# A hybrid decoder block on one core: a fifth pair of gates by seven products, six direct gates as filling, accumulating stores for the heads' second halves, and the keys of the linear attention in ScalarE's queue

## The chip, the cores and the metric

The kernel runs on one core of a Trainium2 chip, in one launch. A core has five engines, each with an instruction queue of its own that is worked off in order: TensorE (PE in the profile; loading its weights is shown apart as PEld), VectorE (DVE), ScalarE (ACT), GpSimd (POOL) and SyncE (SP). DMA transfers are asked for from the queues of SP, ACT and POOL and then run beside the engines. An instruction waits for what it needs by semaphores; all that stands behind it in its queue waits too.

The metric is the device time of the launch in microseconds (us); the number given for a kernel is the median of several runs.

## The reference

One layer of a decoder block on 1024 positions of width 1024, in float32. Cut to what matters here:

```python
xn = rms_norm(h, norm_mix_g)
proj = xn @ w_in                # sb_q, sb_k, sb_v, g_q, g_k, g_v, g_r, g_a, gate_sb, gate_gla
o_sb  = stick_breaking_attention(heads(sb_q, 8), heads(sb_k, 8), heads(sb_v, 8))
o_gla = gla_chunked(heads(g_q, 4) * GLA_DK ** -0.5, heads(g_k, 4), heads(g_v, 4), log_a)
o_gla = rms(o_gla) * gla_norm_g * silu(g_r)
y = (sigmoid(gate_sb + b_gate[0]) * (o_sb @ w_branch_sb)
     + sigmoid(gate_gla + b_gate[1]) * (o_gla @ w_branch_gla))
h = h + y @ w_out
hn = rms_norm(h, norm_ffn_g)
a, g = split(hn @ w_ffn_in)     # 2 x 2816 columns
h = h + (gelu(causal_conv3(a)) * g) @ w_ffn_out
out = rms_norm(h, norm_final_g)
```

The two merge gates (`gate_sb`, `gate_gla`) have 1024 channels each. The kernel holds a projection transposed, 128 channels on the partitions and 1024 positions along, so the gates are 16 blocks of 128 channels; the code calls one such block "a gate". Stick-breaking attention weighs position s for position t by a sigmoid times a product over the positions between, without a softmax. The gated linear attention (GLA) goes in chunks with a state from chunk to chunk; its "keys to the end of the chunk" (`k_to_end`, here `kt`) multiply the values to give the state's increments.

## The kernel before, in words

**Precision.** Each float32 operand of a large matrix product is held as two pieces, a high one of reduced precision and the rest: `split` (L121) is a copy with a cast on ScalarE (L122) and a subtraction on VectorE (`sub`, L113). A product is three matmuls (high by high, high by low, low by high); `mac` (L205 is the matmul in it) issues them for k blocks of 128 rows, into one PSUM bank of 128x512.

**Seven products.** A projection of two blocks of 128 channels can be done by one level of the seven-product scheme: `fast` (L235) takes pairs of channel blocks, builds four differences of their weight quarters, turns seven weight quarters into pieces, does seven products of 4 x 3 = 12 matmuls against prepared sums of `xn` (the dictionary `xq`), and adds the products up on VectorE. Done directly, one gate is 2 halves of the positions x 8 blocks of rows x 3 = 48 matmuls and needs no additions.

**Stages.** By the time at which they run in the profile: (1) load, norm and values, to about 150 us. (2) The pairs of projections by seven products, to about 343 us; their list is `project_pairs` (L589), and its last entries are the gate pairs, `N_GATES`/2 = 4 of them. A gate that is ready goes through a sigmoid and is stored to DRAM (`gate_d`). (3) Stick-breaking attention, `attend` (L883), to about 537 us. (4) GLA, `gated` (L1047), with the first branch projection `branch` (L1072) between its steps, to about 605 us. (5) The second branch, the output projection and the FFN's first product, to about 1290 us. (6) The FFN's second product in four quarters (`phase`, L1334), with the final norm of the last rows in `fourth_done` (L1417).

**Attention and its filling.** For each head `attend` yields blocks of 128x128 weights: `weigh` does the scores on PE, the sigmoid on ScalarE (L830) and a scan on VectorE (L833); `turn_weights` transposes up to four blocks on PE (L842) and splits them into pieces; `gather` multiplies by the values (L871). A gather covers one head and 256 positions, so there are 32, four to a head. Its result has two halves of 64 partitions (from the high and the low piece of the values) that are still to be added. ScalarE moves it out of PSUM with a bias (L877, two rows), and SP stores the two halves to two places of `osb_d` (L879). When the first half of the positions is complete for all heads, `heads` (L847) loads eight tiles back, adds them in pairs on VectorE (L119) and splits the four sums into `ob`, the operand of the first branch projection; for the second half of the positions the same is called inside GLA.

Between the attention's pieces PE is given gates to do directly: `gates` (L686) yields after each group of 6 matmuls, and the loop over `attend` (L1143 on) asks for one such group each time that a number of blocks has been yielded: `FILL` = 6 in the first three quarters of the blocks, 4 in the last. At the end of `attend` a drain empties its queues; there each yield counts for 2 blocks. What is left of the gates runs out after `fetch_rest`, in one go (`fill(gate_steps, 128)`). With `N_GATES` = 8 there are 16 - 8 = 8 gates of this kind. Three of them (`N_HALVES`) have their second halves of the positions done at the very end, and before those three halves `fetch_gated` asks for GLA's values, queries and inverse keys.

**Order around attention's end.** After the loop the program does `branch(0, ...)` up to its first stop, which loads the first two pieces of the branch weights (`in_w_branch_sb_dram`, two DMAs of 512 KB in POOL's queue, L181) and splits them; then `fetch_rest` (L956) loads the keys `kt` for two pairs of heads (L962, 512 KB each, in POOL's queue); then the last gates run. GLA starts with `states`, whose matmul (L970) is the first to read `kt`. The program fixes the order in each engine's queue, except that a priority offset (`LATER`) lets the scheduler that lays out the queues move gate matmuls later. Tiles come from pools with a fixed number of buffers (`t2`: 11 of 128x512; `t4`: 14 of 128x1024), so a new tile waits until the old one in its buffer has been read for the last time.

## Time and profile before

| | |
|---|---|
| median of 3 runs | 1386.93 us (1386.27 to 1387.03) |
| the profiled execution: its time | 1386.67 us |
| the profiled execution: its span | 1384.8 us |
| mean granted TensorE clock | 0.997 |

The page's parts on stages, by windows of the trace (columns: us of the window, then for PE, PEld, DVE, ACT and POOL the busy us and in brackets the number of instructions, the granted TensorE clock, the DMA engines' busy share, GB/s):

```profile
0.00:150.00 150.00, 146.95 (x660) 117.24 (x661) 104.29 (x164) 63.52 (x120) 22.33 (x36) 0.99 0.46 151
150.00:343.40 193.40, 193.40 (x868) 159.94 (x866) 143.48 (x224) 100.77 (x149) 40.02 (x66) 1.00 0.62 184
343.40:537.00 193.60, 192.36 (x1183) 167.00 (x1181) 156.56 (x232) 125.92 (x305) 28.17 (x50) 1.00 0.68 176
537.00:605.00 68.00, 67.99 (x422) 56.20 (x422) 43.61 (x88) 39.24 (x140) 14.19 (x22) 1.00 0.65 210
605.00:1290.00 685.00, 684.15 (x3048) 566.21 (x3048) 554.33 (x832) 267.37 (x438) 27.83 (x52) 1.00 0.49 163
```

How to read what is shown of the profile, here and in the prediction: "L205 PE MATMUL bank<-t,t" is the group of PE's matmuls at line 205 of the kernel, from two tiles named `t` into a PSUM bank; then come the tile's shape, "x" and the count, the busy us, the mean ns of one, and the idle us of the engine just before them with what ended it. In a row of the timeline, the start and the length in us stand first, then the engine ("SPq" is SP's queue), and in square brackets an idle time ahead of it and what released it. The chain of waits follows the work that ended last back to the start. Line numbers are those of the kernel before; behind the changed places, the changed kernel's are lower by 3 to 5 around attention and GLA (L966 of the changed kernel is L970 of the one before, L872 is L877, L958 is L962).

### The profile page before, as it was taken

Reading aid. Unit: us, or ns where it says so; the run is one execution under the profiler, and the core shown is the slowest. Engines: PE = TensorE matmul, PEld = TensorE weight load, DVE = VectorE, ACT = ScalarE, POOL = GpSimd, SP = SyncE. Lnnn points to the kernel's source line nnn. Section 1 sums busy time; section 2 is a strip of 40 time slices with the busy share of each in tenths; the row PEclk is TensorE's granted clock in tenths of the full one; section 3 lists DMA queues with packets and bytes.
Section 4 is the critical chain, followed back from the end, with each engine's and each line's share of the span. In section 5 each row is a group of like instructions: output and inputs, shape, how many; then the busy total and the mean of one; then the engine's idle time right before and its main releaser. Section 6 shows DMA issues by size and latency. Waiting matters only on the chain.

```text
span 1384.8 us, 18329 instructions
## 1 busy us (share of the span) xinstructions
PE 1372.4 (99%) x6559; PEld 1138.8 (82%) x6559; DVE 1064.6 (77%) x1640; ACT 643.9 (46%) x1244; POOL 136.3 (10%) x233
## 2 busy tenths in 40 slices
PE   9999999999999999999999999999999999999997
PEld 6788888888888888888888788888888888888886
DVE  6388688874878877658348998998888977896765
ACT  7334445653766664724126443343333334454654
POOL 2002123101111002200000000000000000000000
PEclk9999999999999999999999999999999999999999
DMA  6335278448776567673325245554444537953332
GB/s 239 132 117 151 84 221 251 143 158 210 216 158 151 131 197 237 198 237 136 136 91 177 52 120 187 196 189 152 150 163 152 182 107 272 322 163 102 99 101 105
DMA packets 164108, 227.92 MB, mean 165 GB/s; under 512 B 10938, under 2 KB 105276, under 8 KB 163506
## 3 DMA queue, kind: packets, MB, share of 16 engines
q1 hardware_dynamic: 134944, 139.01, 33.0%
q0 software_dynamic: 22496, 73.73, 16.8%
q10 hardware_dynamic: 6578, 14.03, 2.7%
q8 instruction: 51, 0.84, 0.3%
q14 instruction: 39, 0.32, 0.1%
HBM read 160.28 MB, written 66.45 MB: 164 GB/s over the span
## 4 chain that ended last, share of the span: by engine, by line
PE 95%; DVE 3%; ACT 1%; issue 0%; DMA 0%; ACTq 0%; DVEq 0%
PE bank L205 58%; PE bank L1343 15%; PE bank L385 6%; PE bank L1210 6%; PE bank L871 3%; PE bank L828 2%; PE bank L842 2%; DVE t L113 2%; PE bank L494 1%; PE bank L340 1%; DVE t L119 1%; PE bank L562 1%; PE bank L1007 1%; PE bank L970 0%; PE bank L994 0%
## 5 line engine op out<-in xcount | busy, mean ns | idle before, releaser
L205 PE MATMUL bank<-t,t 128*128 128x512 f32 x3624 | 861.1, 393 | 0.9 <-DVE t L113 0.7
L205 PEld LDWEIGHTS bank<-t,t 128*128 128x128 f32 x3624 | 676.5, 188 | 143.1 <-DVE t L113 1.6
L113 DVE TENSOR_TENSOR t<-t,t 128x512 fp32r<-128x512 f32 (+3 forms) x655 | 434.6, 697 | 93.5 <-ACT t L122 87.2
L122 ACT CAST t<-t 128x512 fp32r<-128x512 f32 (+1 forms) x543 | 320.3, 627 | 325.4 <-DVE t L113 81.0
L119 DVE TENSOR_TENSOR t<-bank,t 128x512 f32<-128x512 f32 x266 | 179.3, 685 | 97.9 <-PE bank L205 54.9
L1343 PE MATMUL bank<-t,t 128*128 128x512 f32 x924 | 209.6, 389 | 0.0
L1343 PEld LDWEIGHTS bank<-t,t 128*128 128x128 f32 x924 | 173.5, 188 | 36.0
L113 DVE TENSOR_TENSOR t<-bank,t 128x512 fp32r<-128x512 f32 (+4 forms) x124 | 69.5, 574 | 27.5 <-ACT t L122 26.9
L1210 PE MATMUL bank<-t,t 128*128 128x512 f32 x384 | 88.8, 391 | 0.0
L1241 ACT ACTIVATE t<-t,vcol 128x1024 f32<-128x1024 f32 x22 | 27.4, 1245 | 127.5 <-DVE t L119 127.5
L113 DVE TENSOR_TENSOR t<-t 128x512 f32<-128x512 f32 x120 | 83.3, 701 | 4.1 <-DMA t<-in_w_ffn_in_dram 3.7
L1210 PEld LDWEIGHTS bank<-t,t 128*128 128x128 f32 x384 | 71.6, 188 | 14.6
L119 DVE TENSOR_TENSOR t<-t,t 128x512 f32<-128x512 f32 x115 | 75.5, 686 | 9.8 <-ACT t L628 8.6
L122 ACT CAST t<-bank 128x512 fp32r<-128x512 f32 (+3 forms) x120 | 60.3, 512 | 48.8 <-PE bank L842 26.8
L385 PE MATMUL bank<-t,t 128*128 128x512 f32 x336 | 77.9, 391 | 0.0
L385 PEld LDWEIGHTS bank<-t,t 128*128 128x128 f32 x336 | 62.7, 188 | 13.1 <-DVE t L113 0.2
L1243 DVE SCALAR_TENSOR_TENSOR t<-t,vcol,t 128x1023 f32<-128x1023 f32 (+1 forms) x44 | 56.3, 1279 | 14.1 <-ACT t L1241 13.9
L833 DVE TENSOR_TENSOR_SCAN t<-t,t 128x128 f32<-128x128 f32 (+1 forms) x64 | 51.6, 816 | 17.5 <-ACT t L830 17.2
L828 PE MATMUL bank<-t,t 128*128 128x128 f32 (+3 forms) x192 | 54.6, 369 | 0.0
L842 PE MATMUL bank<-ident,t 128*128 128x128 f32 x288 | 53.2, 273 | 0.0
L871 PE MATMUL bank<-t,t 128*128 128x256 f32 (+1 forms) x320 | 51.0, 276 | 1.2 <-ACT t L122 0.7
L830 ACT ACTIVATE t<-bank 128x128 f32<-128x128 f32 (+3 forms) x96 | 46.9, 507 | 7.2 <-DMA osb_d<-t 3.2
(164 smaller groups left out, 813.5 us busy)
## 6 DMA issues: line engine op xcount, KB each, us to landing
t<-in_w_ffn_in_dram SPq DMA_DIRECT2D x50, 512.0 KB, 5.1
t<-in_w_in_dram SPq DMA_DIRECT2D x43, 512.0 KB, 5.3
act_d<-t POOLq DMA_DIRECT2D x22, 512.0 KB, 5.8
t<-in_w_ffn_out_dram SPq DMA_DIRECT2D x22, 512.0 KB, 7.6
wsum_d<-t POOLq DMA_DIRECT2D x22, 512.0 KB, 4.5
t<-act_d SPq DMA_DIRECT2D x22, 512.0 KB, 5.9
t<-wsum_d SPq DMA_DIRECT2D x44, 256.0 KB, 3.1
t<-in_w_ffn_out_dram SPq DMA_DIRECT2D x33, 256.0 KB, 2.7
```

The source lines that it names most:

```text
L113: nc.vector.tensor_tensor(out=o, in0=a, in1=b, op=ALU.subtract)
L119: nc.vector.tensor_tensor(out=o, in0=a, in1=b, op=ALU.add)
L122: nc.scalar.copy(h, src)
L205: nc.tensor.matmul(pt, a[:, kk], b[:, kk], start=start and kk == 0 and m == 0, stop=stop and kk == k - 1 and m == 2)
L385: nc.tensor.matmul(pt, a[:, k % 4, t], b, start=k == 0 and m == 0, stop=k == NK - 1 and m == 2)
L828: nc.tensor.matmul(z[:, 0:w], q[:, a, e, ts_], kk[:, e, b0 * P:b1 * P], start=a == 0, stop=a == 1)
L833: nc.vector.tensor_tensor_scan(out=kr, data0=kr, data1=above[:, 0:w], initial=1.0, op0=ALU.mult, op1=ALU.max)
L842: nc.tensor.transpose(pt[:, b * P:(b + 1) * P], ke[:, b * P:(b + 1) * P], ident)
L871: nc.tensor.matmul(po[:, c0:2 * P], vt[b][:, head, :], a[b // 4][:, b % 4, c0:], start=(b == 0 and n == 0), stop=(b == nb - 1 and n == 1))
L1210: nc.tensor.matmul(pt, a[:, k % 4, t], b, start=(k == 0 and m == 0), stop=(k == NK - 1 and m == 2))
L1243: nc.vector.scalar_tensor_tensor(out=cv[:, i:], in0=av[:, :S - i], scalar=col(V_CW, (2 - i) * NF + f), in1=cv[:, i:], op0=ALU.mult, op1=AL ...
L1343: nc.tensor.matmul(pts[m][i], a[:, t], b, start=(k == 0 and x_ == 0), stop=(k == NH - 1 and x_ == 2))
```

## The change

Five things change together.

1. `N_GATES` goes from 8 to 10: a fifth pair of gates is done by seven products in stage 2, and six gates instead of eight are left for filling.
2. `FILL` goes from (6, 4) to (8, 5), and a yield of the drain counts for `FILL[1]` blocks, so that each is followed by one group of 6 gate matmuls while there are any.
3. The two halves of a gather's result go to the same place of `osb_d`: the first half by a plain store in SP's queue, the second by an accumulating store in POOL's queue, which adds to what the first has written and therefore waits until that one has landed. `heads` loads four tiles instead of eight and adds nothing.
4. The loads of the keys `kt` in `fetch_rest` go from POOL's queue to ScalarE's.
5. In `fourth_done` the squares are written to `spare8`, the products in place, and the output is stored from the rows of `hr`.

```diff
--- before.py
+++ after.py
@@ -36,7 +36,7 @@
 T2 = 11
 AWAKE = 3
 T4 = 14
-FILL = 6, 4
+FILL = 8, 5
 EACH = 0
 LATER = 25
 MORE = 1
@@ -54,7 +54,7 @@
 WAIT = 1, 1, 5, 4, 1
 PACES = 0, 0, 0, 1
 EARLY = 6
-N_GATES = 8
+N_GATES = 10
 AT_END = 51
 HEADS_AT = 2
 GROUP = 4, 2
@@ -847,19 +847,14 @@
     def heads(th):
 
         ob.append(quarter())
-        asked, added = deque(), deque()
+        asked = deque()
         for k in range(6):
             if k < 4:
-                asked.append((t2(), t2()))
-                for n, v in enumerate(asked[-1]):
-                    nc.sync.dma_start(v, osb_d[n * HALF + k * P:n * HALF + (k + 1) * P, th * HALF:(th + 1) * HALF])
+                asked.append(t2())
+                nc.sync.dma_start(asked[-1], osb_d[k * P:(k + 1) * P, th * HALF:(th + 1) * HALF])
             yield
             if k > 1:
-                split(*(a[:, k - 2] for a in ob[th]), added.popleft())
-            if k in range(1, 5):
-                a, b = asked.popleft()
-                add(a, a, b)
-                added.append(a)
+                split(*(a[:, k - 2] for a in ob[th]), asked.popleft())
             yield
 
     def gather(head, tp, ah, al):
@@ -875,8 +870,9 @@
             c = slice(n * P, (n + 1) * P)
             i = head * NT + 2 * tp + n
             nc.scalar.activation(o[:, c], po[:, c], AF.Identity, bias=vend[:, i:i + 1])
-        for n, r in enumerate(HALVES):
-            nc.sync.dma_start(osb_d[n * HALF + head * 64:n * HALF + (head + 1) * 64, tp * 2 * P:(tp + 1) * 2 * P], o[r])
+        dst = osb_d[head * 64:(head + 1) * 64, tp * 2 * P:(tp + 1) * 2 * P]
+        nc.sync.dma_start(dst, o[HALVES[0]])
+        nc.gpsimd.dma_start(dst, o[HALVES[1]], accum_op=ALU.add)
         if head == SBH - 1 and tp == 1:
             first_heads.append(heads(0))
 
@@ -934,7 +930,7 @@
                 gather(*late.popleft())
             for v in first_heads:
                 next(v, None)
-            yield 2
+            yield FILL[1]
         fill(*first_heads, 12)
 
     last_values()
@@ -959,7 +955,7 @@
         state.extend((v[:, 0], v[:, 1]) for v in small)
         for p in range(2):
             kt = t4()
-            nc.gpsimd.dma_start(kt, kt_d[p * P:(p + 1) * P, :])
+            nc.scalar.dma_start(kt, kt_d[p * P:(p + 1) * P, :])
             gla[p] += by(kt, NT), by(t4(), NT)
 
     def states(p, n0, n1):
@@ -1415,23 +1411,21 @@
             mul(row(4 + i, 1), row(4 + i, 1), gfin[0][:, HALF:])
 
     def fourth_done(i, p4):
-        r = row(4 + i, 0)
+        r, q = row(4 + i, 0), row(4 + i, 1)
         sub(r, r, p4)
-        o = spare[i % 2]
         a, b = ss[i]
-        nc.scalar.activation(o[:, :HALF], r, AF.Square, accum_out=b)
+        nc.scalar.activation(spare8[:, i], r, AF.Square, accum_out=b)
         add(a, a, b)
         nc.scalar.activation(b, a, AF.Sqrt, bias=eps, scale=1.0 / D)
         nc.vector.reciprocal(a, b)
-        nc.scalar.activation(o[:, HALF:], row(4 + i, 1), AF.Copy, scale=a)
-        nc.vector.scalar_tensor_tensor(out=o[:, :HALF], in0=r, scalar=a, in1=gfin[0][:, :HALF],
-                                       op0=ALU.mult, op1=ALU.mult)
+        nc.scalar.activation(q, q, AF.Copy, scale=a)
+        nc.vector.scalar_tensor_tensor(out=r, in0=r, scalar=a, in1=gfin[0][:, :HALF], op0=ALU.mult, op1=ALU.mult)
         t = slice((4 + i) * P, (5 + i) * P)
         if i < 3:
-            nc.gpsimd.dma_start(out[t, :], o)
+            nc.gpsimd.dma_start(out[t, :], hr[4 + i])
         else:
-            nc.sync.dma_start(out[t, :HALF], o[:, :HALF])
-            nc.scalar.dma_start(out[t, HALF:], o[:, HALF:])
+            nc.sync.dma_start(out[t, :HALF], r)
+            nc.scalar.dma_start(out[t, HALF:], q)
 
     for n, _ in enumerate(jobs):
         if n == 0:
```

Three places of the queues show what moves. In them "DMASW" in a wait stands for the landing of a transfer that POOL asked for, "DMAHW" for the landing of one that SP or ScalarE asked for, and PE, DVE and Activation for work of TensorE, VectorE and ScalarE.

POOL's queue from the end of attention to GLA's first state, before (`gv_d`, `qd_d` and `ki_d` are the operands that `fetch_gated` loads, `in_w_branch_sb_dram` the branch weights, `kt_d` the keys, L981 the scaling of the first state):

```order
L950 DMA t_965_4971<-gv_d 128x4x512 [waits PE_49]
L952 DMA t_964_4970<-qd_d 128x1024 [waits DMASW4_49,PE_49]
L953 DMA t_964_4970<-ki_d 128x1024 [waits DMASW5_49]
L181 DMA t_1027_5307<-in_w_branch_sb_dram 128x4x256 [waits DMASW6_49,DMAHW6_49,DVE_49,PE_49]
L181 DMA t_1030_5315<-in_w_branch_sb_dram 128x4x256 [waits DMASW7_49,DMAHW0_49,DVE_49,PE_49]
L962 DMA t_1035_5325<-kt_d 128x1024 [waits DMASW0_49,PE_49]
L962 DMA t_1037_5328<-kt_d 128x1024 [waits DMAHW3_49,DMAHW1_49,DMAHW4_49,DMASW1_49,PE_49]
L981 TENSOR_SCALAR t_1036_5327<-t_1033_5323,emid_992 128x128 [waits DVE_49,DMAHW4_49,PE_49,Activation_49]
```

The same place in the changed kernel:

```order
L875 DMA osb_d<-t_984_5051 64x256 [waits DMAHW0_49,DMASW1_49,Activation_49]
L875 DMA osb_d<-t_1005_5135 64x256 [waits DMAHW4_49,DMASW2_49,Activation_49]
L875 DMA osb_d<-t_1023_5235 64x256 [waits DMAHW7_49,DMASW3_49,Activation_49]
L181 DMA t_1032_5320<-in_w_branch_sb_dram 128x4x256 [waits DMASW4_49,DVE_49,PE_49]
L875 DMA osb_d<-t_1025_5257 64x256 [waits DMAHW0_49,DMASW5_49,Activation_49]
L181 DMA t_1035_5328<-in_w_branch_sb_dram 128x4x256 [waits DMASW6_49,PE_49]
L875 DMA osb_d<-t_1031_5313 64x256 [waits DMAHW2_49,DMASW7_49,Activation_49]
L977 TENSOR_SCALAR t_1041_5340<-t_1038_5336,emid_992 128x128 [waits DMAHW5_49,DVE_49,PE_49]
```

The two loads of `kt_d` are gone from here, and the accumulating stores of the last gathers (L875) now stand ahead of, between and behind the two loads of branch weights; each waits for the landing of an SP store of the same gather (t_1025 is the result of the last but one gather, t_1031 that of the last).

ScalarE's queue at the same place, before (t_1027 and t_1030 are the two loads of branch weights, whose casts are L122; t_1026 is the last gather's result; L719 and L720 are a gate's sigmoid and its store):

```order
L122 CAST t_1028_5309<-t_1027_5307 128x512 [waits DMASW6_49]
L122 CAST t_1029_5312<-t_1027_5307 128x512
L877 ACTIVATE t_1026_5294<-bank_5277,t_478_2890 128x128 [waits DMAHW6_49,PE_49]
L877 ACTIVATE t_1026_5294<-bank_5277,t_478_2890 128x128
L719 ACTIVATE t_1039_5343<-bank_5253,vcol 128x512 [waits DMAHW0_49,PE_49]
L122 CAST t_1031_5317<-t_1030_5315 128x512 [waits DMASW7_49]
L122 CAST t_1032_5320<-t_1030_5315 128x512
L720 DMA gate_d<-t_1039_5343 128x512 [waits Activation_49]
```

The same place in the changed kernel (t_1032 and t_1035 are the two loads of branch weights, t_1031 the last gather's result):

```order
L122 CAST t_1033_5322<-t_1032_5320 128x512 [waits DMASW4_49]
L122 CAST t_1034_5325<-t_1032_5320 128x512
L872 ACTIVATE t_1031_5313<-bank_5296,t_500_3028 128x128 [waits DVE_49,PE_49]
L872 ACTIVATE t_1031_5313<-bank_5296,t_500_3028 128x128
L122 CAST t_1036_5330<-t_1035_5328 128x512 [waits DMASW6_49]
L122 CAST t_1037_5333<-t_1035_5328 128x512 [waits DVE_49]
L958 DMA t_1040_5338<-kt_d 128x1024
L958 DMA t_1042_5341<-kt_d 128x1024 [waits DMAHW4_49]
```

The last gate's sigmoid is gone from this stretch, and the loads of the keys stand behind the casts of the second load of branch weights.

PE's queue from the end of the last gather to the first use of the keys, before (t_1035 is a tile of keys):

```order
L871 MATMUL bank_5277<-t_992_5079,t_585_3294 128x128
L205 MATMUL bank_5253<-t_542_3125,t_1005_5143 128x512
L205 MATMUL bank_5253<-t_59_336,t_1006_5146 128x512
L205 MATMUL bank_5253<-t_60_337,t_1006_5146 128x512
L205 MATMUL bank_5253<-t_59_336,t_1006_5146 128x512 x2
L205 MATMUL bank_5253<-t_60_337,t_1006_5146 128x512
L205 MATMUL bank_5253<-t_59_336,t_1006_5146 128x512 x2
L205 MATMUL bank_5253<-t_60_337,t_1006_5146 128x512
L205 MATMUL bank_5253<-t_59_336,t_1006_5146 128x512 x2
L205 MATMUL bank_5253<-t_60_337,t_1006_5146 128x512
L205 MATMUL bank_5253<-t_59_336,t_1006_5146 128x512
L970 MATMUL bank_5350<-t_963_4966,t_1035_5325 128x256 [waits DMASW0_49]
```

In the changed kernel (t_1040 is a tile of keys):

```order
L866 MATMUL bank_5296<-t_1003_5121,t_604_3414 128x256
L866 MATMUL bank_5296<-t_1001_5119,t_604_3414 128x128
L866 MATMUL bank_5296<-t_1003_5121,t_604_3414 128x128
L966 MATMUL bank_5348<-t_926_4822,t_1040_5338 128x256 [waits DMAHW3_49,DMASW5_49,PE_49]
L205 MATMUL bank_5356<-t_989_5073,t_1033_5322 128x512 [waits PE_49,Activation_49]
```

The 13 gate matmuls that stood between the last gather and the first use of the keys are gone; the gates have been used up before, and the first matmul on keys follows the last gather's last matmul.

## The prediction, made before the changed kernel had run

> **What bounds the kernel now.** I read the page's busy shares first, then the waits of PE, then windows of one stage each, then the timeline around the only place where PE waits late.
>
> ```profile
> span 1384.8 us, 18329 instructions
> PE 1372.4 (99%) x6559; PEld 1138.8 (82%) x6559; DVE 1064.6 (77%) x1640; ACT 643.9 (46%) x1244; POOL 136.3 (10%) x233
> PE 95%; DVE 3%; ACT 1%; issue 0%; DMA 0%; ACTq 0%; DVEq 0%
> PE bank L871 <- ACT t L122: 0.7, 1, 0.7
> PE bank L871 <- DVE t L113: 0.5, 1, 0.5
> ```
>
> TensorE (PE) is busy 99% of the span and carries 95% of the chain that ended last. The two waits quoted are the only ones that PE has after the first microseconds, except 0.7 us once: 1.2 us, both in the last two heads' gathers. So time is PE's work plus what a change makes PE wait. The price of a matmul has to be read with care:
>
> ```profile
> L205 PE MATMUL bank<-t,t 128*128 128x512 f32 x3624 | 861.1, 393 | 0.9 <-DVE t L113 0.7
> 1100.00:1200.00 100.00, 100.00 (x443) 82.84 (x442) 78.13 (x115) 39.70 (x63) 3.21 (x6) 1.00 0.63 225
> ```
>
> One 128x512 matmul lasts 393 ns, but 443 of them start in 100 us. They overlap, so one more or less is worth 100/443 = 0.226 us, not 0.393.
>
> **The fifth pair.** Two gates done directly are 96 matmuls (2 halves x 24 x 2 gates); the seven products are 7 x 12 = 84. Twelve fewer, 12 x 0.226 = **-2.7 us** of PE work; the order has the same difference (3624 and 3612 rows of that helper). The pair adds 18 operations of 128x512 to DVE (4 differences, 7 pieces' low halves, 7 additions).
>
> ```profile
> L113 DVE TENSOR_TENSOR t<-t,t 128x512 fp32r<-128x512 f32 (+3 forms) x655 | 434.6, 697 | 93.5 <-ACT t L122 87.2
> ```
>
> 18 x 0.70 = 12.5 us lie under the pair's 84 x 0.226 = 19.0 us of PE: no cost. If that cover were gone, it would be at most the part above 19.0.
>
> **The filling.** 83 matmuls (18.8 us) leave attention: two gates fewer there, and what is left of them ends sooner.
>
> ```profile
> 378.00:388.90 10.90, 10.90 (x65) 9.25 (x64) 10.89 (x15) 7.18 (x16) 3.39 (x7) 1.00 0.79 163
> 416.00:423.00 7.00, 7.00 (x47) 6.10 (x46) 7.00 (x11) 5.73 (x15) 0.00 (x0) 1.00 0.14 30
> sum 193.60, PE 192.36 PEld 167.00 DVE 156.56 ACT 125.92 POOL 28.17; mean PE 32.06 PEld 27.83 DVE 26.09 ACT 20.99 POOL 4.70
> who waited for it (us, times):
>   ACT t L830: 3.2, 4
> ```
>
> The sum is attention from 343.4 to 537.0. DVE is 156.6 of 193.6 busy now. It loses 8 additions and 4 pieces, 12 x 0.70 = 8.4, so afterwards 148 of 175, 85% instead of 81%. On average that fits under PE, but the two windows shown have DVE at 10.89 of 10.90 and 7.00 of 7.00: with less filling PE waits there. The last two lines are from the view of the tensor osb_d: ScalarE's sigmoid has waited 3.2 us, in 4 places, for the buffer of an output that was still being stored. The accumulating store keeps that buffer for a second transfer, behind the first. I take **+1.0** for both, bounds 0 and +6 (the 3.2 three times over, less what PE's lead hides).
>
> **The end of attention** is the term that decides. Before:
>
> ```profile
> 527.46 1.17 PE L871 MATMUL bank<-t,t 128*128 128x256 f32 x9
> 528.47 0.62 PE L842 MATMUL bank<-ident,t 128*128 128x128 f32 x4
> 528.85 0.48 PE L205 MATMUL bank<-t,t 128*128 128x512 f32 x1
> 529.17 1.03 PE L842 MATMUL bank<-ident,t 128*128 128x128 f32 x8
> 529.96 1.40 PE L205 MATMUL bank<-t,t 128*128 128x512 f32 x5
> 532.06 0.39 PE L871 MATMUL bank<-t,t 128*128 128x256 f32 x1 [0.71 <-ACT t L122]
> 532.28 1.31 PE L205 MATMUL bank<-t,t 128*128 128x512 f32 x5
> 533.44 1.89 PE L871 MATMUL bank<-t,t 128*128 128x256 f32 x15
> 535.16 3.19 PE L205 MATMUL bank<-t,t 128*128 128x512 f32 x13
> 538.20 0.59 PE L970 MATMUL bank<-t,t 128*128 128x256 f32 x2
> 528.82 1.17 POOL L962 DMA_DIRECT2D t<-kt_d  x2 [0.36 <-PE bank L871]
> ```
>
> From the end of the gather of head 6 (528.5) to the first matmul that uses the keys kt (L970, 538.2) PE has 9.7 us, with 24 gate matmuls in it; the keys were asked for at 528.8, at the stretch's beginning. In the changed order only 6 gate matmuls stand in this stretch. PE's work there is 12 transposes (528.47 to 529.96 less one matmul, 1.26), 16 gather matmuls at 1.72/15 = 0.115 (1.84) and 6 x 0.226 (1.36): 4.5 us.
>
> And the keys are asked for much later. In ScalarE's queue their two DMAs stand behind the casts of the second branch-weight load; that load stands in POOL's queue behind the accumulating store of head 6; that store waits until the plain store of the same bytes has landed. So a chain runs from the end of head 6's gather to the keys' landing. Its rows:
>
> ```profile
> 535.37 0.63 ACT L877 ACTIVATE t<-bank,t 128x128 f32<-128x128 f32 x2 [2.32 <-PE bank L871]
> 536.02 1.08 SPq L879 DMA_DIRECT2D osb_d<-t  x2
> 531.86 1.19 ACT L122 CAST t<-t 128x512 fp32r<-128x512 f32 x2
> DMA to landing us min/median/max: 1.9/4.4/8.4
> t<-in_w_branch_sb_dram POOLq DMA_DIRECT2D x2, 512.0 KB, 4.5
> t<-kt_d POOLq DMA_DIRECT2D x2, 512.0 KB, 6.3
> t<-in_w_branch_gla_dram SPq DMA_DIRECT2D x4, 512.0 KB, 4.0
> ```
>
> Evacuation: matmuls end at 533.44 + 1.89 = 535.33, the store is issued at 536.02, 0.7. Store's landing (the fourth line, of osb_d): 1.9 to 4.4, I take 2.5, near the lower end, since heads' loads no longer crowd this moment. The accumulating store's issue on POOL: 1.17/2 = 0.6. The weights' landing: 4.5. Two casts: 1.1. The keys' landing: between 4.0 (a load of this size on a hardware queue) and 6.3 (on POOL); 4.5, nearest to the hardware queue that they now use. Sum 0.7 + 2.5 + 0.6 + 4.5 + 1.1 + 4.5 = 13.9. PE has 4.5 us to do, so it idles 9.4; bounds from the ends: 0.7 + 1.9 + 0.6 + 3.9 + 1.1 + 4.0 = 12.2 and 0.7 + 4.4 + 0.6 + 5.2 + 1.1 + 6.3 = 18.3, idle 7.7 to 13.8 (for the weights I put 3.9 and 5.2: 4.5 less and more 0.7). The old 1.2 us of waits in this stretch go. Net **+8.2**.
>
> No row shows an accumulating store; nothing here waits for its landing, only for its issue, so that unknown is within the +1.0 above. The Trainium skill, DMA: Bandwidth & Descriptors, section "Anatomy of one DMA", gives a POOL transfer 2.0 us plus bytes at 436 GB/s, and puts most of the 2.0 on the receipt of the written bytes. By it the weights would take 3.2 us instead of the row's 4.5, and as an estimate the idle time would be 1.3 shorter; the rows decide.
>
> **The clock.**
>
> ```profile
> 6.00:8.00 2.00, 0.65 (x5) 0.50 (x6) 1.70 (x4) 1.20 (x3) 0.00 (x0) 1.00 1.04 417
> 8.00:10.00 2.00, 2.00 (x7) 1.45 (x8) 1.83 (x3) 1.98 (x4) 0.80 (x1) 0.57 1.05 395
> 10.00:12.00 2.00, 2.00 (x6) 1.11 (x6) 1.97 (x4) 1.97 (x6) 2.00 (x2) 0.57 1.05 409
> 1382.00:1384.80 2.80, 0.00 (x0) 0.00 (x0) 0.00 (x0) 0.00 (x0) 0.00 (x0) 0.50 0.30 110
> ```
>
> After 6 to 8 us, when PE was mostly idle, the granted clock (the eighth number) is 0.57 over 4 us: 4 x 0.43/0.5 = 3.4 us at half speed, 1.7 us lost; and it is 0.50 at the end, with PE idle. A wait of 9 us must show the same: **+1.7**, bounds 0 and 3.4. The Trainium skill (TensorE: Matmul & The Clock Gate, "The HAM clock gate") asks for a whole idle window of about 3.4 us before the clock halves; here 1.35 us of idle in one 2 us window were enough. By either, 9 us of idle time suffice and 1.2 us cost nothing more, so the sum stays.
>
> **The rest.** Heads' additions leave DVE and ScalarE's wait for them; SP has fewer transfers; both counted. The last rows' squares and products write into other tiles, with the same operations in the same chain: 0. A fallback of the keys' or queries' prefetch behind POOL's accumulating stores is within the +1.0.
>
> **Sum** against the profiled execution (1386.67 us with its span of 1384.8, 0.3 below the median of 1386.93): 1386.7 - 2.7 + 1.0 + 8.2 + 1.7 = 1394.9, **1395.0 us**. With every bound low it is 1386.7 - 2.7 + 0 + 6.5 + 0 = 1390.5, with every bound high 1386.7 - 2.7 + 6 + 12.6 + 3.4 = 1406.
>
> **Rivals.**
> - *The keys come in time* (the other side, faster). Place: the same first use of kt. If store, weights and keys land before PE asks, PE loses nothing: 1386.7 - 2.7 - 1.2 = 1382.8. It decides where the chain is shorter than 4.5 + 3.9 = 8.4 us: below this the change is faster. Against it: two 512 KB loads and a store follow each other, 3.9 + 4.0 + 1.9 = 9.8 even at the lowest rows. For it: only an error in who waits for whom. 11%.
> - *Only part of the wait*: the chain takes 8 to 11 us, the clock stays up: 1384 to 1389, say 1387. It needs all lowest rows at once. 7%.
> - *Attention itself becomes the bound*: the held buffers and the full DVE make PE wait more than 6 us besides: 1395 + 9 = 1404. For it: DVE at 100% in the windows above, and POOL queues 32 more transfers, each behind a store's landing, with the next heads' keys behind them. Against it: PE waits nowhere there now. 10%.
> - That the change does not do what it says is excluded: the order has the 84 and the missing 96.
>
> **How the numbers follow.** Forecast 72% (1390.5 to 1403), rivals 11, 7, 10. A measurement of this kernel tells about 0.2% (2.8 us) from no change. Faster by more: the first rival, 0.11. Same: the second, 0.07. Slower: 0.82. The range leaves out the first rival and most of the third's upper half: 1386 to 1403.
>
> **What would show it.** In the changed profile: PE's first matmul of kt (L966) with an idle time of 8 to 14 us before it, released by a DMA from kt_d; POOL's second branch-weight load issued 3 to 5 us after head 6's store; a granted clock near 0.5 for some 3 us behind the wait; L205 12 fewer. Wrong is the reading if that wait is under 4 us, or if PE waits more in attention than at its end.

## The result, and the profile after the change

The changed kernel takes **1405.17 us** (median of 4 runs, 1404.88 to 1407.26) against 1386.95 for the kernel before: a ratio of 1.0136 (95% interval 1.0118 to 1.0153), 18.2 us slower. Forecast were 1395.0, 8.2 us slower, and at most 1403. The profiled execution took 1405.04 us with a span of 1403.1.

The page's head of the changed kernel, and its chain of waits by engine:

```profile
span 1403.1 us, 18319 instructions
PE 1374.8 (98%) x6547; PEld 1139.5 (81%) x6547; DVE 1065.9 (76%) x1646; ACT 645.3 (46%) x1246; POOL 163.2 (12%) x263
PE 65%; DVE 3%; DMA 2%; issue 1%; ACT 1%; POOL 0%; ACTq 0%; POOLq 0%; DVEq 0%
```

PE has 12 matmuls fewer and is busy 2.4 us longer, and the chain that ended last now has DMAs in it, 2% of the span, where the kernel before had 0%. (The chain could be followed back only to about 385 us, so its shares add up to 72%.) The waits of PE (us in total, times, longest) tell where:

```profile
PE bank L966 <- DMA t<-kt_d: 10.8, 1, 10.8
PE bank L828 <- ACT t L830: 3.2, 1, 3.2
PE bank L866 <- DVE t L113: 1.0, 2, 0.8
PE bank L828 <- DMA t<-sqkl_d: 0.9, 1, 0.9
```

The first is the forecast wait for the keys. The others, in attention, were not forecast at this size. To place the whole 18.3 us of the span I cut both executions at the same instructions. Of the kernel before, from PE's timeline: attention's first score matmul (L828) and the end of the matmuls; the last gather's end (535.33) and the first matmul on keys (538.20) stand in the prediction:

```profile
343.43 0.73 PE L828 MATMUL bank<-t,t 128*128 128x128 f32 x4
1369.71 7.87 PE L1343 MATMUL bank<-t,t 128*128 128x512 f32 x34
```

and the same four places of the changed kernel:

```profile
362.52 0.73 PE L828 MATMUL bank<-t,t 128*128 128x128 f32 x4
540.16 1.99 PE L866 MATMUL bank<-t,t 128*128 128x256 f32 x15
552.91 1.19 PE L966 MATMUL bank<-t,t 128*128 128x256 f32 x2 [10.77 <-DMA t<-kt_d]
1379.66 14.44 PE L1339 MATMUL bank<-t,t 128*128 128x512 f32 x63
```

| part | before | after | difference | forecast |
|---|---|---|---|---|
| to attention's first matmul (the fifth pair) | 343.43 | 362.52 | +19.1 | +19.0 |
| attention, to the last gather's end | 191.90 | 179.63 | -12.3 | -19.0 (83 matmuls -18.8, filling +1.0, old waits -1.2) |
| from there to the first matmul on keys | 2.87 | 10.77 | +7.9 | +6.5 (9.4 idle for 13 matmuls) |
| to the last matmul (half clock) | 839.38 | 841.20 | +1.8 | +1.7 |
| to the end of the span | 7.23 | 9.03 | +1.8 | 0 |
| sum | 1384.8 | 1403.1 | +18.3 | +8.2 |

Two rows carry the error: attention, 6.7 us, and the end behind the last matmul, 1.8. The wait for the keys adds 1.4.

**The wait for the keys.** The chain named in the prediction, in its timeline rows: PE's gather of head 6, ScalarE's evacuation, the accumulating store, the second branch weights, the keys:

```profile
536.12 0.93 PE L866 MATMUL bank<-t,t 128*128 128x256 f32 x7
537.09 0.63 ACT L872 ACTIVATE t<-bank,t 128x128 f32<-128x128 f32 x2 [2.85 <-PE bank L866]
541.83 0.83 POOL L875 DMA_DIRECT2D osb_d<-t  x1 [3.98 <-ACT t L122]
542.37 1.10 POOL L181 DMA_DIRECT2D t<-in_w_branch_sb_dram  x1
547.09 0.81 ACTq L958 DMA_DIRECT2D t<-kt_d  x2
```

From the gather's end at 537.05 to the accumulating store 4.8 us (forecast 0.7 + 2.5), to the weights' load 0.5 (0.6), to the keys' loads 4.7 (4.5 + 1.1: the DMAs are issued while the first cast runs, so the casts cost nothing), to the landing 5.8 (4.5). That is 15.9 for 13.9; PE had 5.1 us to do for 4.5, and idled 10.8 for 9.4.

**The clock.** Windows of the same place (the eighth number is the granted clock):

```profile
546.00:548.00 2.00, 0.00 (x0) 0.00 (x0) 0.27 (x1) 0.92 (x2) 0.84 (x1) 0.51 0.94 328
554.00:556.00 2.00, 2.00 (x6) 1.56 (x5) 0.58 (x2) 0.41 (x1) 0.37 (x1) 0.50 0.88 280
```

PE works again from 552.9 and is still at half clock in the second window, with 6 matmuls in 2 us: the 1.8 us of the table's fourth row.

**Attention's longest wait.** A window of the stretch before it, the landing of the stores to `osb_d` from 490 to 506 (minimum, median, maximum), and rows of SP, POOL, ScalarE and PE:

```profile
495.00:500.00 5.00, 5.00 (x31) 4.20 (x30) 1.67 (x3) 3.22 (x9) 0.21 (x1) 1.00 1.00 388
DMA to landing us min/median/max: 2.5/3.8/6.5
492.69 0.45 SPq L874 DMA_DIRECT2D osb_d<-t  x1
499.79 0.87 POOL L875 DMA_DIRECT2D osb_d<-t  x1 [6.15 <-ACT t L872]
504.68 0.77 ACT L830 ACTIVATE t<-bank 128x128 f32<-128x128 f32 x2 [4.69 <-issue]
505.01 0.78 PE L828 MATMUL bank<-t,t 128*128 128x512 f32 x1 [3.17 <-ACT t L830]
```

The sigmoid L830 at 504.68 writes into the buffer that held a gather's result. By the program's semaphores it waits for that result's two stores. The plain one, issued at 492.69, took the 6.5 us that are the maximum here and landed at 499.2; in that time GLA's loads of 2 MB were under way, and from 495 to 500 the DMA engines were 100% busy. So the accumulating store was issued only at 499.79 (its row names ScalarE, but the semaphores that it waits for are those of the stores), and it landed at 504.6. ScalarE, and behind it VectorE and PE, stood still.

### The profile page after: what moved, and what is told of

Its sections match the earlier page's. It is cut to its first block, busy times and chain, and to the rows that moved or that the text cites. A ratio compares the mean times of both kernels' runs of the same rounds, so it can differ in the third digit from the quotient of the medians.

```text
span 1403.1 us, 18319 instructions
## 1 busy us (share of the span) xinstructions
PE 1374.8 (98%) x6547; PEld 1139.5 (81%) x6547; DVE 1065.9 (76%) x1646; ACT 645.3 (46%) x1246; POOL 163.2 (12%) x263
## 4 chain that ended last, share of the span: by engine, by line
PE 65%; DVE 3%; DMA 2%; issue 1%; ACT 1%; POOL 0%; ACTq 0%; POOLq 0%; DVEq 0%
PE bank L205 38%; PE bank L1339 15%; PE bank L1206 5%; PE bank L866 2%; DVE t L113 2%; PE bank L828 2%; PE bank L842 1%; DMA osb_d<-t 1%; DMA t<-sqkl_d 1%; DVE t L119 1%; PE bank L1003 1%; PE bank L966 0%; DMA t<-kt_d 0%; DMA t<-in_w_branch_sb_dram 0%; PE bank L990 0%
## 5 line engine op out<-in xcount | busy, mean ns | idle before, releaser
L205 PE MATMUL bank<-t,t 128*128 128x512 f32 x3612 | 856.4, 393 | 0.9 <-DVE t L113 0.8
L205 PEld LDWEIGHTS bank<-t,t 128*128 128x128 f32 x3612 | 675.7, 188 | 142.6 <-DVE t L113 1.6
L122 ACT CAST t<-t 128x512 fp32r<-128x512 f32 (+1 forms) x546 | 322.2, 627 | 322.7 <-DVE t L113 80.1
L119 DVE TENSOR_TENSOR t<-bank,t 128x512 f32<-128x512 f32 x273 | 183.7, 684 | 106.8 <-PE bank L205 63.8
L122 ACT CAST t<-bank 128x512 fp32r<-128x512 f32 (+3 forms) x120 | 59.9, 514 | 38.9 <-PE bank L340 17.4
L119 DVE TENSOR_TENSOR t<-t,t 128x512 f32<-128x512 f32 x107 | 70.0, 684 | 9.4 <-ACT t L628 8.6
L1239 DVE SCALAR_TENSOR_TENSOR t<-t,vcol,t 128x1023 f32<-128x1023 f32 (+1 forms) x44 | 56.2, 1278 | 14.1 <-ACT t L1237 13.9
L828 PE MATMUL bank<-t,t 128*128 128x128 f32 (+3 forms) x192 | 54.8, 372 | 4.1 <-ACT t L830 3.2
L830 ACT ACTIVATE t<-bank 128x128 f32<-128x128 f32 (+3 forms) x96 | 47.5, 509 | 17.7 <-DMA gate_d<-t 5.3
L1243 POOL DMA_DIRECT2D act_d<-t x22 | 11.7, 531 | 352.5 <-DVE t L116 352.5
```

Of the source, the lines that this page charges most:

```text
L119: nc.vector.tensor_tensor(out=o, in0=a, in1=b, op=ALU.add)
L122: nc.scalar.copy(h, src)
L205: nc.tensor.matmul(pt, a[:, kk], b[:, kk], start=start and kk == 0 and m == 0, stop=stop and kk == k - 1 and m == 2)
L828: nc.tensor.matmul(z[:, 0:w], q[:, a, e, ts_], kk[:, e, b0 * P:b1 * P], start=a == 0, stop=a == 1)
L830: nc.scalar.activation(ke[:, 0:w], z[:, 0:w], AF.Sigmoid, scale=-SBD ** -0.5)
L1239: nc.vector.scalar_tensor_tensor(out=cv[:, i:], in0=av[:, :S - i], scalar=col(V_CW, (2 - i) * NF + f), in1=cv[:, i:], op0=ALU.mult, op1=AL ...
```

## The experiments

Each run was timed beside the kernel before, whose median was 1386.9 to 1387.0 in all of them. "Attention" is the time from the first score matmul to the last gather's end, "keys" PE's wait for kt, "clock" the time from the first matmul on keys to the last matmul, "end" from there to the end of the span, all from the profiled execution.

| run | median us | ratio (95%) | attention | keys | clock | end |
|---|---|---|---|---|---|---|
| before | 1386.95 | | 191.9 | 0 | 839.4 | 7.2 |
| after | 1405.17 | 1.0136 (1.0118 to 1.0153) | 179.6 | 10.8 | 841.2 | 9.0 |
| pair_alone | 1389.24 | 1.0018 (1.0009 to 1.0028) | 177.5 | 0.4 | 839.9 | 7.2 |
| accumulate_alone | 1399.55 | 1.0090 (1.0075 to 1.0105) | 190.8 | 8.4 | 841.1 | 10.1 |
| keys_alone | 1397.67 | 1.0077 (1.0062 to 1.0092) | 191.9 | 7.9 | 841.1 | 7.8 |
| no_accumulate | 1394.54 | 1.0052 (1.0036 to 1.0069) | 177.7 | 3.7 | 842.0 | 7.1 |
| no_pair | 1397.55 | 1.0073 (1.0058 to 1.0089) | 190.9 | 6.8 | 842.1 | 9.0 |
| branch_on_sp | 1400.36 | 1.0099 (1.0081 to 1.0117) | 177.6 | 5.5 | 841.1 | 8.9 |
| keys_on_sp | 1401.99 | 1.0108 (1.0093 to 1.0124) | 179.0 | 6.3 | 841.8 | 9.0 |
| own_buffers | 1404.55 | 1.0130 (1.0114 to 1.0146) | 179.2 | 11.5 | 841.1 | 9.4 |
| second_half_by_pool | 1396.30 | 1.0069 (1.0053 to 1.0085) | 191.9 | 4.8 | 841.8 | 9.4 |
| pair_refilled | 1389.77 | 1.0021 (1.0011 to 1.0030) | 177.0 | 0.5 | 840.0 | 6.8 |
| pair_fewer_sums | 1387.29 | 1.0003 (0.9994 to 1.0013) | 175.1 | 0 | 840.3 | 7.2 |
| pair_helped | 1397.66 | 1.0078 (1.0062 to 1.0094) | 179.9 | 4.6 | 841.0 | 6.8 |
| pair_pieces_by_pool | 1392.32 | 1.0034 (1.0020 to 1.0049) | 180.8 | 0 | 841.5 | 6.8 |
| pair_pieces_sums_by_pool | 1397.35 | 1.0075 (1.0060 to 1.0090) | 179.1 | 0.3 | 844.6 | 6.9 |
| rows_by_sp | 1386.37 | 0.9997 (0.9988 to 1.0007) | 191.9 | 0 | 839.4 | 7.0 |
| before_pieces_by_pool | 1386.85 | 0.9998 (0.9989 to 1.0007) | 192.0 | 0 | 839.3 | 7.0 |

### The parts of the change, alone and left out

**pair_alone**

```diff
-FILL = 6, 4
+FILL = 8, 5
-N_GATES = 8
+N_GATES = 10
-            yield 2
+            yield FILL[1]
```

> The kernel before with the fifth pair, the new filling rate and the drain's yield, and nothing else. My theory (what costs time is the accumulating stores and the place of the keys' loads, not the thinner filling): PE's work falls by 2.7 us, attention has waits of under 1.5 us, the keys are asked for at the end of the last but one gather and PE waits 0 to 2 us for them: 1383 to 1387 us. Rival (the thinner filling itself makes attention wait): attention waits of 4 us or more and 1388 us or more.

The rival holds. Attention should lose 83 x 0.2267 = 18.8 us and loses 14.4 (191.9 to 177.5): the thinner filling costs 4.4 us, more than the 2.7 that the seven products save, and the kernel is 2.3 us slower. The waits of PE that the trace names in attention make 3.0 of the 4.4 us; the rest is not placed. The longer of them, and two windows with VectorE (third pair of numbers) full:

```profile
PE bank L871 <- DVE t L113: 1.8, 3, 0.8
PE bank L828 <- DVE t L113: 0.8, 1, 0.8
385.00:389.00 4.00, 3.19 (x20) 2.54 (x19) 4.00 (x8) 1.63 (x6) 0.34 (x2) 1.00 1.01 364
530.00:534.00 4.00, 3.41 (x21) 2.80 (x20) 4.00 (x6) 0.78 (x3) 1.58 (x3) 1.00 0.75 218
```

**accumulate_alone**

```diff
-        for n, r in enumerate(HALVES):
-            nc.sync.dma_start(osb_d[n * HALF + head * 64: ...], o[r])
+        nc.sync.dma_start(dst, o[HALVES[0]])
+        nc.gpsimd.dma_start(dst, o[HALVES[1]], accum_op=ALU.add)
```

(with the shorter `heads`)

> The kernel before with the accumulating stores and the shorter heads alone. My theory: attention waits 4 to 6 us for buffers that the accumulating stores hold, POOL's drain at the end is 8.1 us instead of 6.3, since it grows with POOL's transfers (1.8 us later end), and the keys' wait is 1 to 4 us (they stand behind accumulating stores in POOL's queue): 1393 to 1399 us. Rival (only thin filling makes the held buffers felt): no waits in attention above those of before, only the 1.8 us: 1387 to 1389 us.

For attention the rival holds: it is 1.1 us shorter than before, not 4 to 6 longer. With the old filling the held buffers cost nothing. The time, 1399.55, lies above both ranges all the same: the end is longer by 2.9, and the wait for the keys is 8.4, twice my upper end. They still are in POOL's queue there; timeline:

```profile
538.22 0.83 POOL L875 DMA_DIRECT2D osb_d<-t  x1 [3.96 <-DMA osb_d<-t]
538.76 1.42 POOL L958 DMA_DIRECT2D t<-kt_d  x2
545.95 1.22 PE L966 MATMUL bank<-t,t 128*128 128x256 f32 x2 [8.36 <-DMA t<-kt_d]
```

POOL waits 4 us for the plain store of the last gather, then for the accumulating store's issue, and only then asks for the keys, 10 us later than before (528.82).

**keys_alone**

```diff
-            nc.gpsimd.dma_start(kt, kt_d[p * P:(p + 1) * P, :])
+            nc.scalar.dma_start(kt, kt_d[p * P:(p + 1) * P, :])
```

> The kernel before with the keys' loads in ScalarE's queue alone. My theory: there they stand behind the last gate's sigmoid and the casts of the second branch-weight load, are asked for at about 539 instead of 528.8, and PE waits 5 to 7 us for them, with 1 to 2 us of half clock behind: 1392 to 1396 us. Rival (the accumulating store ahead of the branch weights alone makes that wait): within 1 us of the kernel before.

My theory holds in kind, but was undersized: the wait is 7.9 us and the kernel 10.8 us slower, both above the ranges given. ScalarE asks for the keys as soon as it starts the last gate's sigmoid, which waits for the last gate matmul:

```profile
538.74 0.69 ACT L719 ACTIVATE t<-bank,vcol 128x512 f32<-128x512 f32 x1 [2.40 <-PE bank L205]
538.75 0.82 ACTq L962 DMA_DIRECT2D t<-kt_d  x2
546.61 1.19 PE L970 MATMUL bank<-t,t 128*128 128x256 f32 x2 [7.91 <-DMA t<-kt_d]
```

So moving two DMAs into another queue costs 10.8 us by itself; the landing took 7.9 here.

**no_accumulate** is the changed kernel with the first diff above and the old `heads` taken back.

> The changed kernel with both halves stored by SP, heads with eight loads and additions, the rest as changed. My theory: attention's waits fall from 5 us to under 1.5, the drain is back at 6.3 us, and the keys are asked for at the end of the last gather, so PE waits 5 to 7 us for them instead of 10.8: 1390 to 1395 us. Rival (thin filling): attention waits stay at 4 us or more and the time stays above 1397 us. Rival (the keys' wait is made by the accumulating stores alone): that wait is under 2 us and the time under 1387 us.

The keys' wait falls from 10.8 to 3.7, more than expected: the weights are there early, and ScalarE asks for the keys as soon as the end of the last gather releases its evacuation, at 540.58. Of attention's waits 4.6 us stay (177.7 against 191.9 - 18.8 = 173.1): they belong to the thin filling, as pair_alone says, not to the stores, and in that the first rival holds. The time lies in the range of my theory by luck: a wait for the keys shorter than expected makes up for the waits that stay in attention. The end is back at 7.1.

**no_pair** is the changed kernel with pair_alone's diff taken back.

> The changed kernel with four pairs of gates by seven products, eight direct gates and the old filling; the accumulating stores, the keys' queue and the last rows stay as changed. My theory (in attention the thin filling costs 4.4 us, and the accumulating stores' 3.2 us wait near 501 comes only together with it): attention has waits of under 1 us, the keys' wait is 7 to 10 us, the end keeps POOL's long drain: 1397 to 1401 us. Rival (the accumulating stores alone make attention wait): 4 us or more of waits in attention and 1402 us or more.

My theory holds: no wait in attention, 6.8 us at the keys (a little below the 7 to 10), the long end. So neither alone makes the wait of 3.2 us near 501: in accumulate_alone and no_pair it is not there, in pair_alone neither. In numbers for attention: +4.4 by the filling, -1.1 by the accumulating stores, +6.5 together, so the parts do not add up. The accumulating stores also take the heads' additions away, and without those of the first heads the thin filling costs only 2.0 us (pair_fewer_sums below: 175.1 against 173.1). The other 4.5 of the 6.5 come only of both: the wait of 3.2 us and the half clock behind it, 10 us at a granted 0.83, which is 1.7 us (4.9 together).

### The chain to the keys

**branch_on_sp**

```diff
-                    raws[:] = [load(w[...], 4, None, nc.gpsimd if b == 0 and i < m else None)]
+                    raws[:] = [load(w[...], 4, None, None)]
```

> The changed kernel with the first two branch-weight loads in SP's queue, so that no accumulating store stands ahead of them. My theory (a chain: store, its landing, accumulating store, weights, casts, keys): without the store's landing in the chain the weights are asked for right behind the store of the last but one gather, the casts run when the last gather is out, and the keys are asked for some 4 us earlier: PE's wait for them falls from 10.8 to 6 to 8 us, 1400 to 1402 us. Rival (the keys' own transfer and the buffers that they need set the time): the wait stays above 9.5 us and the time within 1.5 us of the changed kernel.

```profile
536.10 1.11 SPq L181 DMA_DIRECT2D t<-in_w_branch_sb_dram  x2
541.71 0.33 ACTq L958 DMA_DIRECT2D t<-kt_d  x1
545.47 1.19 PE L966 MATMUL bank<-t,t 128*128 128x256 f32 x2 [5.50 <-DMA t<-kt_d]
```

The second load of weights is asked for 5.6 us earlier, the keys 5.4, and PE waits 5.5 instead of 10.8 us, somewhat less than I expected. The median falls by 4.8 us, as expected. (The profiled execution is this kernel's fastest, 1397.28; near 501 PE waits 1.5 us in it, where the changed kernel's has 3.2.)

**keys_on_sp** has `nc.sync.dma_start(kt, ...)` in the changed kernel.

> The changed kernel with the keys' loads in SP's queue. There they stand behind the plain store of the last gather, which waits for nothing but ScalarE. My theory (the place in the queue sets when the keys are asked for): asked for 3 to 4 us earlier than in the changed kernel, PE waits 5 to 8 us at their first use or, right behind it, for the branch weights' pieces: 1399 to 1403 us. Rival (the crowd of transfers sets their landing): the keys land no more than 1 us earlier, 1404 us or more.

The keys are asked for at 543.10 instead of 547.09, PE waits 6.3 us, and the median falls by 3.2. Asked for 4.0 us earlier, they shorten the wait by 4.5: the place in the queue sets it, as forecast.

### Attention: buffers, filling, VectorE

**own_buffers**

```diff
-T2 = 11
+T2 = 9
-        o = t2()[:, 0:2 * P]
+        o = sb.tile([P, 2 * P], F32, tag="ho", name=nm("ho"), bufs=4)
```

> The changed kernel with the gathers' results in four buffers of their own of half the size, and two buffers fewer in the pool of the sigmoids. My theory (the sigmoid at 504.7 waits for the buffer of a gather's result that the accumulating store still reads): PE's wait of 3.2 us near 501 and the half clock behind it go, and nothing else moves by much: 1399 to 1402 us. Rival (thin filling or the crowd of loads makes that wait): a wait of 2 us or more stays within 10 us of that place, and the time is above 1403 us.

```profile
PE bank L966 <- DMA t<-kt_d: 11.5, 1, 11.5
PE bank L866 <- DVE t L113: 1.7, 2, 0.9
PE bank L828 <- DMA t<-sqkl_d: 1.5, 2, 1.0
PE bank L828 <- ACT t L830: 0.6, 1, 0.6
```

The wait for ScalarE falls from 3.2 to 0.6, so the buffer was its cause. But the time does not fall (1404.55): other waits are longer, 0.6 at the landing of the attention's operands (sqkl_d), 0.7 at VectorE, 0.7 at the keys (its profiled execution, 1407.06, is its slowest). The half clock has moved too: behind the two waits for the operands, 0.5 and 1.0 us at 406.6 and 408.2, the granted clock is 0.83 from 403 to 413, where the changed kernel has 1.00. And attention's first matmul comes 1.6 us later (364.17), with a wait of 0.8 us at 281 that the changed kernel does not have. The expectation on the time failed. Whether the two buffers fewer for the sigmoids made these waits was not tried.

**pair_refilled** deals the gate groups out by 6, 10, 10, 5 blocks in the four quarters of attention:

```diff
-        rate = FILL[done > 3 * NT * (NT + 1) // 2 * SBH // 4]
+        rate = (6, 10, 10, 5)[min(3, (done - 1) // (NT * (NT + 1) // 2 * SBH // 4))]
```

It also has the new last rows, with their stores in SP's queue.

> The kernel before with the fifth pair, the new last rows, the last output stores in SP's queue, and the six direct gates dealt out by 6 blocks in the first quarter of attention, 10 in the middle half and 5 in the last quarter instead of 8, 8 and 5. My theory (the pair alone lost its gain to waits for a full VectorE where the filling is thin, first near 387): the waits near 387 and 393, 1.4 us, go, at most 1 us comes in the middle half, and the end is 0.4 us earlier: 1386 to 1389 us. Rival (VectorE's total work in attention is the bound, wherever the filling stands): within 0.7 us of pair_alone's 1389.2.

The rival holds: 1389.77 against pair_alone's 1389.24. The waits up to 420, 1.5 us, are gone, and 1.8 us have come between 430 and 505; only those behind 523 are shorter, 0.5 for 1.5, in an execution that is this kernel's fastest (1388.16).

**pair_fewer_sums** is pair_alone's kernel and leaves out the additions of the first heads:

```diff
-                add(a, a, b)
+                if th:
+                    add(a, a, b)
```

> The kernel of pair_alone without the four additions of the first heads: the second halves of the results for the first 512 positions are loaded but left out of the sum. My theory (with thin filling PE waits wherever VectorE is full): the waits from 523 on, 2.2 us in pair_alone, fall under 0.5 us, the earlier ones (387 to 457, 2.4 us) stay as they are, and the time is 1386.5 to 1388 us. Rival (the waits come from the thin filling's order itself, not from VectorE's load): within 0.7 us of pair_alone's 1389.2.

My theory holds: 2.8 us less on VectorE, attention 2.4 us shorter, 1.95 us less in all, and no wait between 523 and the last gather but one of 0.1 us. With pair_refilled this says that in attention with the thin filling VectorE's work sets the pace where it is dense. Of the 4.4 us, 2.0 stay, with waits near 389, 394 and 419; what would remove those was not found.

Four runs tried to give VectorE's work to GpSimd. **pair_helped** gives it the low halves of the values' pieces and the first heads' additions:

```diff
-                split(v2[:, i, :, 0:SBD], v2[:, i, :, SBD:P], ...)
+                nc.scalar.copy(h, v)
+                nc.gpsimd.tensor_tensor(out=l, in0=v, in1=h.bitcast(F32), op=ALU.subtract)
-                add(a, a, b)
+                (nc.vector if th else nc.gpsimd).tensor_tensor(out=a, in0=a, in1=b, op=ALU.add)
```

> A version meant to be faster than both: the kernel before with the fifth pair, the new filling and the new last rows, the last output stores in SP's queue, and two groups of VectorE's operations given to GpSimd: the low halves of the values' pieces (8) and the additions of the first heads (4). My theory (pair_alone lost 5 us to waits for a full VectorE, and POOL's drain sets the end): half of these waits go, 1384 to 1387 us. Rival (GpSimd is too slow at them, or holds its loads back): as pair_alone or slower, 1389 us or more.

**pair_pieces_by_pool** gives GpSimd instead the low halves of the direct gates' weight pieces (`piece` in `gates`).

> The kernel before with the fifth pair and the new filling, the new last rows with the last output stores in SP's queue, and the low halves of the direct gates' weight pieces (14 operations of 128x512, 0.7 us each on VectorE, some 1.6 us on GpSimd) on GpSimd. My theory (with thin filling PE waits where VectorE is full): 10 us less VectorE work in attention, its waits fall from 5 to 2 us or less, 1385 to 1387 us. Rival (GpSimd, or the loads behind it in its queue, come too late): 1389 us or more.

**pair_pieces_sums_by_pool** joins that with the additions.

> As pair_pieces_by_pool, with the first heads' four additions on GpSimd too and the first two branch-weight loads in SP's queue, so that they don't wait behind GpSimd's additions. My theory: the waits from 523 on go as well, 1384.5 to 1386.5 us, unless the keys' loads, still in POOL's queue, come late by the additions. Rival: they do, with 3 us or more of wait at the keys, 1388 us or more.

**before_pieces_by_pool** does the pieces so in the kernel before.

> The kernel before, four pairs and the old filling, with the low halves of the direct gates' pieces on GpSimd and the last rows as in rows_by_sp. My theory (with thick filling VectorE's load costs PE only 1.6 us): 1385 to 1386.5 us. Rival (the thick filling hides VectorE everywhere): as rows_by_sp, 1386.4 us.

With the fifth pair all three take 3.1 to 8.4 us more than pair_alone, as the rivals said; without it nothing is gained. In pair_helped the additions also stand in POOL's queue ahead of the keys' loads (4.6 us at the keys). In pair_pieces_sums_by_pool the keys come in time (0.3), against its rival's reason: there PE waits 3.0 us at 545.9 for ScalarE, which waits for the branch weights, now loaded in SP's queue. Timeline of pair_helped, GpSimd's subtractions and VectorE's scans beside them, then PE; and the scans' groups in pair_alone (busy, mean ns):

```profile
368.08 3.14 POOL L820 TENSOR_TENSOR t<-t,t 128x512 fp32r<-128x512 f32 x2 [1.09 <-ACT t L819]
368.38 6.68 DVE L835 TENSOR_TENSOR_SCAN t<-t,t 128x256 f32<-128x256 f32 x4
372.01 4.13 POOL L820 TENSOR_TENSOR t<-t,t 128x512 fp32r<-128x512 f32 x2 [0.78 <-ACT t L819]
377.87 0.56 PE L873 MATMUL bank<-t,t 128*128 128x256 f32 x3 [2.19 <-DVE t L113]
L833 DVE TENSOR_TENSOR_SCAN t<-t,t 128x512 f32<-128x512 f32 x16 | 19.5, 1220 | 10.1 <-ACT t L830 10.1
L833 DVE TENSOR_TENSOR_SCAN t<-t,t 128x384 f32<-128x384 f32 x16 | 15.2, 950 | 2.4 <-ACT t L830 2.4
L833 DVE TENSOR_TENSOR_SCAN t<-t,t 128x256 f32<-128x256 f32 x16 | 10.9, 681 | 1.3 <-ACT t L830 1.1
```

The timeline's row names only the first scan's shape; the four are one of 128x256, two of 128x384 and one of 128x512. They take 6.7 us beside GpSimd's subtractions, and 0.68 + 2 x 0.95 + 1.22 = 3.8 alone. VectorE loses 2.9 us while GpSimd does four subtractions, which on VectorE would take 4 x 0.70 = 2.8: nothing is taken off it. The Trainium skill, "SBUF — State Buffer", section "SBUF: two separate sides", says that a VectorE operation with two SBUF inputs and a GpSimd operation that reads SBUF share one pair of ports, which the one that starts first holds for its whole instruction; the trace agrees.

### The end

**second_half_by_pool**

```diff
-            nc.sync.dma_start(osb_d[n * HALF + head * 64: ...], o[r])
+            (nc.gpsimd if n else nc.sync).dma_start(osb_d[n * HALF + head * 64: ...], o[r])
```

> The kernel before with the second halves stored plainly, to their own rows, but from POOL's queue: 32 more POOL transfers, none that adds. My theory (POOL's last drain grows with the number of POOL's transfers): the drain behind the last output store is 8.0 to 8.4 us instead of 6.3, the end 1.8 us later, and the keys, which then stand behind the last plain store in POOL's queue, make PE wait 2 to 5 us: 1391 to 1396 us. Rival (only transfers that add lengthen the drain): drain 6.2 to 6.4 us.

My theory holds: the drain, shown below, takes 8.14 us although nothing is added. The keys' wait is 4.8 us, and the time lies just above the range.

**rows_by_sp** has the new `fourth_done` with

```diff
-            nc.gpsimd.dma_start(out[t, :], hr[4 + i])
+            nc.sync.dma_start(out[t, :], hr[4 + i])
```

> The kernel before with the new last rows and the last output stores of fourth_done in SP's queue, so that POOL's last transfer, and with it its drain, comes some 7 us or more earlier. My theory (behind the last landing the end waits for POOL's drain): the time from the last matmul to the end falls from 7.2 to 6.8 us and the whole by 0.4 us, 1386.3 to 1386.8 us. Rival (the end waits for SP's landings alone): no change of that time.

The trace's list of all instructions has, behind the kernel's last line, a DRAIN on POOL, which starts with POOL's last store; the program ends 0.8 us after it (1.1 in second_half_by_pool). Start, end:

```
before               POOL DRAIN 1377.69 1384.04   6.35 us   181 transfers from POOL
after                POOL DRAIN 1394.22 1402.36   8.14 us   211
keys_alone           POOL DRAIN 1388.47 1394.65   6.18 us   179
accumulate_alone     POOL DRAIN 1388.08 1396.38   8.30 us   213
second_half_by_pool  POOL DRAIN 1385.44 1393.58   8.14 us   213
```

In the changed kernel the last output has landed at 1399.9 and the drain lasts until 1402.4. It grows by about (8.14 - 6.18) / 32 = 0.06 us for each transfer that POOL has issued in the whole program, adding or plain. All 18 kernels fit this, from 5.93 us with 176 transfers (pair_pieces_sums_by_pool) to 8.30 with 213. Whether the number of transfers counts or that of the rows in them was not tried. In rows_by_sp POOL has issued its last transfer 29 us before the end, and the end is 0.3 us shorter (7.2 to 7.0); the whole, 1386.37, cannot be told from the kernel before.

The new last rows do remove something: in keys_alone and accumulate_alone, which have the old ones, ScalarE waits for the landing of an earlier store from the same buffer; accumulate_alone:

```profile
1385.33 0.63 ACT L1418 ACTIVATE t<-t 128x512 f32<-128x512 f32 x1 [2.11 <-DMA out_dram<-t]
```

Without that wait it idles 1.20 us at this place, so 0.9 us are lost. The changed kernel has no such wait, and the kernel before has none either.

## Where the prediction was right and where it was wrong

The way and the main cause were right; the size was not: 18.2 us slower for 8.2, above the range. Of the 10.1 us that the sum lacks, 6.7 lie in the filling's term, 1.8 in an end put at 0 and 1.4 in the wait for the keys.

- **Right: the direction and its main cause.** The change is slower by a wait of PE at its first matmul on the keys, which comes of a chain through store, accumulating store, branch weights and keys. It was forecast at 9.4 us and is 10.8, inside 7.7 to 13.8; branch_on_sp and keys_on_sp cut the chain at two places and shorten the wait by 5.3 and 4.5. Of its legs the plain store, the weights and the keys were taken too short, by 1.6, 0.2 and 1.3 us; the casts, 1.1, were none. The signs that the prediction named came too: a wait of 8 to 14 us released by a DMA from kt_d, half clock for some 3 us behind it, 12 matmuls of L205 fewer, and less waiting in attention than at its end.
- **Right: the pair itself** (+19.1 for +19.0 ahead of attention) and **the clock** (+1.8 for +1.7). That the clock came out so close is in part luck: in no_accumulate and no_pair, with shorter waits for the keys, the same stretch is 2.6 and 2.7 us longer than before.
- **Wrong: the filling.** The step "I take +1.0 for both, bounds 0 and +6", with the old waits of 1.2 gone, made -0.2; measured is +6.5, so 7.7 for the term itself, over its upper end. The prediction named both parts, the full VectorE and the held buffer, but worked out a price for neither: VectorE's mean load, 85%, seemed to fit under PE. (Four of the eight additions that it counted as gone from attention stand in GLA; VectorE's time there, 148.9 us, came out near its 148 even so.) The runs show: the thin filling alone costs 4.4 us (pair_alone), and 2.0 without the first heads' additions (pair_fewer_sums); the other 4.5 come with the accumulating stores, and only with the thin filling (accumulate_alone and no_pair have no such wait): PE's wait of 3.2 us behind the held buffer and half clock behind that. The buffer is shown as the cause of that wait (own_buffers), but a kernel that gets the 4.5 us back is not: there waits and half clock came elsewhere. The rival "attention itself becomes the bound", given 10%, is nearer than the forecast: it asked for more than 6 us in attention and put 9 there, where 6.5 were lost. That its 1404 is so close to 1405.17 is partly luck, since it had the end at 0 too.
- **Wrong: the end at 0.** The prediction reckoned with the last rows' chain alone, and from the last matmul to the last output's landing nothing changed: 5.8 us before and after. The 1.8 us are POOL's drain, longer by the 32 accumulating stores some 850 us earlier less the two loads of keys. The page shows no drain; the list of all instructions of the kernel before has it, 6.35 us long and ending 0.8 us before the program.
- **Wrong in "nothing here waits for its landing, only for its issue"** of the accumulating store: for the buffers something did, at 504.68.

Waits at the keys do not add up over the parts: 8.4 by the stores alone, 7.9 by the queue alone, 6.8 by the two, 10.8 with the pair. Each change puts another instruction last ahead of the keys' loads, and the pair takes away the gate matmuls under which they could have landed.

## What to carry to other kernels

Filling that keeps TensorE busy also gives the other engines time: before it is thinned, look at windows of 5 to 10 us and price a wait wherever another engine is full in them; here the mean load hid 4.4 us. Of a transfer that is moved to another queue ask which instruction stands last ahead of it there, and what that one waits for; here two DMAs in another queue cost 10.8 us with nothing else changed. An accumulating store makes all that stands behind it in its queue wait for the landing of the plain store, and keeps its source's buffer for two transfers; put no load that is needed soon behind it.
